# Where the first sums of the down weights stand in the gate/up tiles of a Winograd feed-forward kernel

## The chip, the cores and the metric

The kernel runs as one program on one core of a Trainium2 chip. The metric is the device time of one execution in microseconds (us); the time quoted for a kernel is the median of its runs. TensorE (PE in the profile) does the matrix products, VectorE (DVE) and GpSimd (POOL) do elementwise work, ScalarE (ACT) does copies and activation functions, and SyncE (SP) issues nearly all of the loads and stores. Each engine has one queue and works through it in order; an instruction whose data is not there holds up all that stand behind it on its engine.

## The reference

Two layers (DEPTH = 2) of a hybrid encoder, on 1040 tokens (16 meta tokens and 1024), width 1024, in float32. Each layer is a mixer (gated DeltaNet heads and short convolutions) and then a SwiGLU feed-forward block. Only the second is touched here:

```python
def swiglu(h, w_gate_up, w_down):
    gate, up = jnp.split(h @ w_gate_up.astype(h.dtype), 2, axis=-1)
    return (jax.nn.silu(gate) * up) @ w_down.astype(h.dtype)

for l in range(DEPTH):
    h = h + hybrid_mixer(rmsnorm(h, norm1_w[l]), ...)
    h = h + swiglu(rmsnorm(h, norm2_w[l]), w_gate_up[l], w_down[l])
h = rmsnorm(h, final_norm_w)
return h[:, N_META:]
```

The inner width D_FF is 2816, or 22 tiles of 128 (FT = 22).

## The kernel before

**Number format and products.** Every float32 operand is split into a high part `hi` (rounded to fp32r, by ACT) and a low part `lo` (the rest, by DVE or POOL), and a product is three matmuls per 128 x 128 block: hi x hi, hi x lo, lo x hi. Both feed-forward products are done with one level of Winograd's form of Strassen's method: seven products of half size in place of eight, with sums and differences of weight blocks on one side and of activation blocks on the other.

**Gate/up stage.** The loop `for f in range(FT)` (from L1279) makes one of 22 rows of the inner activation per turn; such a turn is called a tile here. A tile loads four weight blocks of 128 x 512: A11 and A12 into `raw` buffers (2 in all), A21 and A22 into `rw` buffers (tag `ck2`, 5 buffers in all), L1281 to L1284. DVE makes s1t = A21 + A22 (L1289), s2t = s1t - A11 (L1290), then s2t = A12 - s2t (L1293) and A21 = A11 - A21 (L1294); s1t and s2t take `ck2` buffers as well. `w_op` splits each of the seven operands (ACT at L1047, POOL at L1048) into a ring of seven slots. PE does the seven products (p1 to p7, L1065 to L1067); DVE takes the results out of the banks at L1313 (p5), L1324 (p3), L1327 (p6), L1331 (p7) and L1340 (p4). The row is then finished: POOL multiplies the gate by the norm factor (L1354), DVE multiplies up by it (L1355), ACT does the silu (L1356), DVE does the last product (L1357), SP stores the row (L1358), and for rows 4 to 12 DVE makes a difference that SP stores too (L1360, L1361). In layer 0 a product is done in two halves of 260 columns, in layer 1 (the last) in one piece of 512. Tiles 0 to 3 have had two of their products done ahead and do the other five.

**First sums of the down weights.** The down product, which comes next, needs for twelve blocks n = 0 to 11 (128 x 384) the Winograd sum S1 = A21 + A22 of the down weights, then S2 and S3 made from it in place. The S1 sums are done while gate/up runs. `s_under(f)` stands in tile f after the `w_op` calls: tiles 8 to 17 have one sum each (n = f - 8), tile 21 has n = 10 and 11. It calls `s_sum("S1", ...)`, which issues two loads of 192 KB (`a_load`, L1130) into a room and the DVE addition into the sum's home (L1156).

- For n < 8 the room is the two halves of one row, `dw["S", 4]`; all eight sums use it, one after another.
- For n of 8 and above the first load goes to the sum's own home and the second (called o below) to a `ck2` buffer.
- The homes: n = 0 to 5 are in the rows of tag `Y[1]` which held the gate rows of tiles 0 to 2; n = 6, 7 are in a `c` buffer which held a row of tile 3; n = 8, 9 are in `dw["S", 4]` itself; n = 10, 11 are in the row that holds the gate of tile 20.

**What sets the order.** Nothing is placed in the queues by hand. The framework lists the program, and a scheduler that plays a timeline of its own fills each engine's queue: among the instructions whose inputs and buffers are free in that timeline it takes the one that stands first in the program. So an instruction can be put far ahead of its place in the program when nothing it needs holds it back. `after(a, b)` adds a dependency of a on b, and with it a bound on how early a can be taken. The dependencies are kept on the chip by semaphores; the order within each queue is fixed.

Of the kernel before, what the change touches and what calls it, by code (L numbers as in the profile page):

```python
# [11 lines left out]
ALU = mybir.AluOpType  # L12
# [8 lines left out]
FT = 22  # L21
# [21 lines left out]
def trunk(ctx: ExitStack, tc: tile.TileContext, xT, w_in, w_ba, w_out, w_gu, w_dn,  # L43
# [8 lines left out]
    def nm(p):  # L52
        cnt[0] += 1
        return f"{p}_{cnt[0]}"
# [4 lines left out]
    def row(tag, dt=F32, bufs=1):  # L59
        return sb.tile([128, L], dt, tag=tag, bufs=bufs, name=nm(tag))  # L60

    def t2k(tag):
        return sb.tile([128, 4, 128], F32, tag="ck2", bufs=5, name=nm(tag))
# [25 lines left out]
    def after(ins, prev):  # L89

        if prev is not None:
            tc.add_manual_dep(ins.ins, prev.ins.name, dep, reason="order")
        return ins
# [6 lines left out]
    tt = nc.vector.tensor_tensor  # L100
# [116 lines left out]
    S = [(("a0", "a1", "a2"), "a3"), (("b0", "b1", "b2"), "b3")]  # L217
# [62 lines left out]
    for l in range(DEPTH):  # L280
# [788 lines left out]
        def raw4(tag):  # L1069
            if tag == "raw":  # L1070
                return wp.tile([128, WK, 128], F32, tag="raw", bufs=2, name=nm("raw"))
            return t2k("rw")
# [43 lines left out]
        dw, held = {}, {}  # L1116
        at, read_out = [0], {}

        def behind(ins):

            return after(ins, read_out.get(at[0] - 2))
# [6 lines left out]
        def a_load(to, dh, fh, n):  # L1128
            f0 = NF + NP * fh + 3 * (n // 4)
            dma(to.rearrange("p (k e) -> p k e", k=3), w_dn[l, 4 * dh + n % 4, :, f0:f0 + 3, :])  # L1130
            return to
# [11 lines left out]
        def s_room():  # L1143

            nr[2] += 1
            r = nr[2] // 2 % 4
            if ("X", r) not in dw:
                dw["X", r] = row(X[1], F32, 3) if r < 3 else row(Y[1] + "f")
            return dw["X", r][:, 384 * (nr[2] % 2):384 * (nr[2] % 2) + 384]

        def s_sum(which, n, room=None):

            S = s_raw(n)
            if which == "S1":
                r, o = room or (s_room(), s_room())
                tt(out=S, in0=a_load(r, 1, 0, n), in1=a_load(o, 1, 1, n), op=ALU.add)  # L1156
            elif which == "S2":
                behind(tt(out=S, in0=S, in1=a_load(s_room(), 0, 0, n), op=ALU.subtract))
            else:
                behind(tt(out=S, in0=a_raw(1, 1, n), in1=S, op=ALU.subtract))  # L1160

        def s_under(f):

            if f == FT - 1:
                ns = (10, 11)
            else:
                ns = (f - 8,) if 0 <= f - 8 < 10 else ()
            for n in ns:
                S = s_raw(n)
                if n == 0:  # L1170
                    s_raw(6)
                    s_raw(8)
                if n < 8:
                    s_sum("S1", n, (dw["S", 4][:, 0:384], dw["S", 4][:, 384:768]))
                else:
                    s_sum("S1", n, (S, raw4("ck2").rearrange("p a b -> p (a b)")[:, 0:384]))

        def w_unit(u):

# [71 lines left out]
        for n in range(12):  # L1251
            under[n + 3].append(lambda n=n: s_sum("S2", n))
            under[n + 49].append(lambda n=n: s_sum("S3", n))
# [25 lines left out]
        for f in range(FT):  # L1279
# [16 lines left out]
            for n, a in ([("S3", A21), ("A22", A22), ("S4", s2t), ("A12", A12)] if end else  # L1296
                         [("S4", s2t), ("S3", A21), ("A12", A12), ("A22", A22)]):
                if f >= NE or n != "A12":
                    W[n] = w_op(a)
            s_under(f)  # L1300
            g, u = early[f] if f < NE else (row((X[1], Y[1])[f % 2] + "f"), row(X[1], F32, 3))
            ps = {}

# [49 lines left out]
            gv, uv, rv = g[:, o0:L], u[:, o0:L], ss[:, o0:L]  # L1353
            ptt(out=gv, in0=gv, in1=rv, op=ALU.mult)  # L1354
            tt(out=uv, in0=uv, in1=rv, op=ALU.mult)  # L1355
            act(out=gv, in_=gv, func=AF.Silu)  # L1356
            tt(out=uv, in0=uv, in1=gv, op=ALU.mult)  # L1357
            dma(ad[f][:, o0:L], uv)  # L1358
            if NF <= f < NF + NP:
                tt(out=gv[:, 0:NB].rearrange("p (g e) -> p g e", g=2), in0=half(uv, 1), in1=half(uv, 0), op=ALU.subtract)  # L1360
# [46 lines left out]
        for u, (p, b, m) in enumerate(UNITS):  # L1407
# [16 lines left out]
            for j in range(NJ):  # L1424
# [9 lines left out]
                if b == NBK - 1:  # L1434
                    dh, z, op = TO[p]
# [138 lines left out]
```

## Time and profile before

| what | us |
|---|---|
| median of 3 runs | 2581.15 |
| lowest, highest of these | 2574.96, 2581.61 |
| the profiled execution, its time | 2581.81 |
| the profiled execution, its span | 2580.0 |
| mean granted TensorE clock | 0.992 |
| layer 0: first and last store of a finished row (L1358) | 676.0, 1098.8 |
| layer 1: first and last store of a finished row (L1358) | 1956.1, 2356.1 |
| layer 0: S1 sums n = 0 to 7 on DVE (L1156) | 676.3 to 728.3 |
| layer 1: the same | 1957.7 to 2013.2 |
| layer 0: S1 sums n = 8, n = 9 start | 949.4, 970.2 |
| layer 1: S1 sums n = 8, n = 9 start | 2212.2, 2231.9 |

The table gives times from the span's start except in its first five rows. In the rows of a view, the first number is the start in us, the second the time taken, then the engine, the line, the operation, output and inputs with their shapes; in square brackets stands how long the engine had been idle before it and what it had waited for. SPq, PEq and so on are the engines' queues (loads, stores, semaphores). Names are those of the buffers: `a` and `b` are the large buffers of the two halves of the memory plan, which change their part from layer to layer; `rw` is a `ck2` buffer.

### The profile page before, as it was taken

The numbers are of one execution on the slowest core, as the hardware profiler recorded it, in microseconds if no ns is written. First come the engines' busy times: TensorE is split into PE (matmuls) and PEld (weight loads), VectorE is DVE, ScalarE is ACT, GpSimd is POOL, SyncE is SP. The second block draws the span as 40 slices with busy tenths as digits, with TensorE's granted clock in tenths as the row PEclk, the third lists the DMA queues.
The fourth block names the chain that finished last, engine by engine and source line by source line (L and its number), as shares of the span: only waits on it lengthen the run. The fifth ranks groups of instructions, "written<-read, shape, count | busy, mean of one in ns | idle before, by whom it ended". The sixth has DMA issues, their size and how long they took to land. (4 is left out here: it accounts for less than half of the span.)

```text
span 2580.0 us, 45319 instructions
## 1 busy us (share of the span) xinstructions
PE 2501.8 (97%) x17508; PEld 2284.7 (89%) x17508; DVE 1660.6 (64%) x2461; ACT 1045.1 (41%) x1945; POOL 1138.4 (44%) x869
## 2 busy tenths in 40 slices
PE   8999999999999999999999998999998999999998
PEld 6989899998899999999998987999977778887787
DVE  4678423648766666678656884235597776768664
ACT  5664232435233333444445742224452333334444
POOL 2141212325666666655420312212466676675663
PEclk9999999999999999999999999999999999999999
DMA  3445665524432222574323556556343322228631
GB/s 127 137 154 171 210 190 165 195 75 130 136 109 87 88 82 81 193 233 140 96 92 122 173 169 209 171 166 204 106 135 115 117 90 94 87 88 268 188 119 70
DMA packets 213764, 360.04 MB, mean 140 GB/s; under 512 B 25460, under 2 KB 87868, under 8 KB 213548
## 3 DMA queue, kind: packets, MB, share of 16 engines
q1 hardware_dynamic: 180300, 310.17, 36.6%
q10 hardware_dynamic: 31072, 42.61, 5.3%
q0 software_dynamic: 2176, 4.36, 0.5%
q8 instruction: 137, 2.24, 0.4%
q14 instruction: 79, 0.65, 0.1%
HBM read 266.60 MB, written 90.46 MB: 138 GB/s over the span
## 5 line engine op out<-in xcount | busy, mean ns | idle before, releaser
L131 POOL TENSOR_TENSOR wlo<-raw,whi 128x512 fp32r<-128x512 f32 x132 | 176.8, 1341 | 760.1 <-ACT whi L130 666.3
L157 PE MATMUL pacc<-a,whi 128*128 128x346 f32 (+1 forms) x808 | 263.9, 330 | 8.8 <-ACT whi L130 6.5
L159 PE MATMUL pacc<-a,wlo 128*128 128x346 f32 (+1 forms) x808 | 264.8, 329 | 0.5 <-DVE wlo L131 0.3
L157 PE MATMUL pacc<-b,whi 128*128 128x346 f32 (+2 forms) x672 | 235.4, 351 | 0.1
L159 PE MATMUL pacc<-b,wlo 128*128 128x346 f32 (+2 forms) x672 | 233.2, 348 | 0.2 <-POOL wlo L131 0.2
L158 PE MATMUL pacc<-a,whi 128*128 128x346 f32 (+1 forms) x688 | 227.1, 330 | 0.6 <-DVE a L178 0.3
L130 ACT ACTIVATE whi<-raw 128x512 fp32r<-128x512 f32 x168 | 105.2, 628 | 277.3 <-PE pacc L158 158.6
L158 PE MATMUL pacc<-b,whi 128*128 128x346 f32 (+2 forms) x580 | 200.9, 347 | 0.3 <-DVE b L906 0.3
L1048 POOL TENSOR_TENSOR wlo<-rw,whi 128x512 fp32r<-128x512 f32 x92 | 134.7, 1466 | 71.8 <-ACT whi L1047 70.4
L157 PEld LDWEIGHTS pacc<-a,whi 128*128 128x128 f32 x808 | 153.4, 191 | 13.2 <-ACT whi L130 8.2
L159 PEld LDWEIGHTS pacc<-a,wlo 128*128 128x128 f32 x808 | 154.2, 191 | 2.1 <-POOL wlo L131 0.5
L157 PEld LDWEIGHTS pacc<-b,whi 128*128 128x128 f32 x672 | 127.1, 189 | 12.0 <-issue 3.1
L158 PEld LDWEIGHTS pacc<-a,whi 128*128 128x128 f32 x688 | 131.4, 191 | 5.2 <-issue 3.3
L1048 POOL TENSOR_TENSOR a<-rw,a 128x512 fp32r<-128x512 f32 x64 | 105.5, 1651 | 68.3 <-ACT a L1047 68.2
L159 PEld LDWEIGHTS pacc<-b,wlo 128*128 128x128 f32 x672 | 127.3, 190 | 9.4 <-issue 0.8
L1048 POOL TENSOR_TENSOR b<-rw,b 128x512 fp32r<-128x512 f32 x64 | 92.4, 1446 | 84.2 <-ACT b L1047 50.1
L158 PEld LDWEIGHTS pacc<-b,whi 128*128 128x128 f32 x580 | 109.8, 189 | 7.5 <-DVE b L906 0.6
L1047 ACT ACTIVATE whi<-rw 128x512 fp32r<-128x512 f32 x92 | 57.8, 630 | 144.4 <-DVE rw L1293 82.5
L1294 DVE TENSOR_TENSOR rw<-raw,rw 128x512 f32<-128x512 f32 x44 | 98.9, 2247 | 1.2
L1289 DVE TENSOR_TENSOR rw<-rw,rw 128x512 f32<-128x512 f32 x44 | 68.2, 1550 | 48.2 <-POOL wlo L1048 30.9
L1048 POOL TENSOR_TENSOR wlo<-raw,whi 128x512 fp32r<-128x512 f32 x50 | 79.0, 1583 | 32.5 <-ACT whi L1047 32.2
L1047 ACT ACTIVATE b<-rw 128x512 fp32r<-128x512 f32 x64 | 40.3, 630 | 122.3 <-PE pacc L1066 35.2
(970 smaller groups left out, 8439.3 us busy)
## 6 DMA issues: line engine op xcount, KB each, us to landing
raw<-in_w_in SPq DMA_DIRECT2D x112, 256.0 KB
raw<-in_w_gu SPq DMA_DIRECT2D x104, 256.0 KB
rw<-in_w_gu SPq DMA_DIRECT2D x88, 256.0 KB
rw<-in_w_dn SPq DMA_DIRECT2D x94, 192.0 KB
rec<-aqd SPq DMA_DIRECT2D x62, 256.0 KB
rec<-vkd SPq DMA_DIRECT2D x61, 256.0 KB
raw<-in_w_out SPq DMA_DIRECT2D x48, 256.0 KB
b<-ad SPq DMA_DIRECT2D x45, 260.0 KB
```

The costliest lines, as they stand in the source:

```text
L130: whi_done[0] = act(out=hi, in_=raw[:, 0:kk, :], func=AF.Copy)
L131: (tt if lov[0] else ptt)(out=lo, in0=raw[:, 0:kk, :], in1=hi.bitcast(F32), op=ALU.subtract)
L157: mm(ps[:, :n], wh, xh[:, n0:n1], start=(k == 0), stop=False)
L158: mm(ps[:, :n], wh, xl[:, n0:n1], start=False, stop=False)
L159: mm(ps[:, :n], wl, xh[:, n0:n1], start=False, stop=(k == K - 1))
L1047: act(out=hi, in_=src, func=AF.Copy)
L1048: ptt(out=lo, in0=src, in1=hi.bitcast(F32), op=ALU.subtract)
L1289: tt(out=s1t, in0=A21, in1=A22, op=ALU.add)
L1294: tt(out=A21, in0=A11, in1=A21, op=ALU.subtract)
```

## The change

The S1 addition is taken out of `s_sum` and put behind the row. `s_under(f)` keeps the place of the two loads in the program (after the tile's `w_op` calls, ahead of its products) and hands back a list of the additions. These are traced after the row's last product (L1357 of before), with a dependency on it (`row_done`); in tile 21 the dependency is on the last product of row 20 (`row_before`). The rooms, the homes, the number of loads and the number of additions are the same.

```diff
--- before.py
+++ after.py
@@ -1148,13 +1148,10 @@
                 dw["X", r] = row(X[1], F32, 3) if r < 3 else row(Y[1] + "f")
             return dw["X", r][:, 384 * (nr[2] % 2):384 * (nr[2] % 2) + 384]
 
-        def s_sum(which, n, room=None):
+        def s_sum(which, n):
 
             S = s_raw(n)
-            if which == "S1":
-                r, o = room or (s_room(), s_room())
-                tt(out=S, in0=a_load(r, 1, 0, n), in1=a_load(o, 1, 1, n), op=ALU.add)
-            elif which == "S2":
+            if which == "S2":
                 behind(tt(out=S, in0=S, in1=a_load(s_room(), 0, 0, n), op=ALU.subtract))
             else:
                 behind(tt(out=S, in0=a_raw(1, 1, n), in1=S, op=ALU.subtract))
@@ -1165,15 +1162,20 @@
                 ns = (10, 11)
             else:
                 ns = (f - 8,) if 0 <= f - 8 < 10 else ()
+            adds = []
             for n in ns:
                 S = s_raw(n)
                 if n == 0:
                     s_raw(6)
                     s_raw(8)
                 if n < 8:
-                    s_sum("S1", n, (dw["S", 4][:, 0:384], dw["S", 4][:, 384:768]))
+                    r, o = dw["S", 4][:, 0:384], dw["S", 4][:, 384:768]
                 else:
-                    s_sum("S1", n, (S, raw4("ck2").rearrange("p a b -> p (a b)")[:, 0:384]))
+                    r, o = S, raw4("ck2").rearrange("p a b -> p (a b)")[:, 0:384]
+                a_load(r, 1, 0, n)
+                a_load(o, 1, 1, n)
+                adds.append((S, r, o))
+            return adds
 
         def w_unit(u):
 
@@ -1297,7 +1299,7 @@
                          [("S4", s2t), ("S3", A21), ("A12", A12), ("A22", A22)]):
                 if f >= NE or n != "A12":
                     W[n] = w_op(a)
-            s_under(f)
+            adds = s_under(f)
             g, u = early[f] if f < NE else (row((X[1], Y[1])[f % 2] + "f"), row(X[1], F32, 3))
             ps = {}
 
@@ -1354,7 +1356,10 @@
             ptt(out=gv, in0=gv, in1=rv, op=ALU.mult)
             tt(out=uv, in0=uv, in1=rv, op=ALU.mult)
             act(out=gv, in_=gv, func=AF.Silu)
-            tt(out=uv, in0=uv, in1=gv, op=ALU.mult)
+            row_done = tt(out=uv, in0=uv, in1=gv, op=ALU.mult)
+            for to, r, o in adds:
+                after(tt(out=to, in0=r, in1=o, op=ALU.add), row_done if f < FT - 1 else row_before)
+            row_before = row_done
             dma(ad[f][:, o0:L], uv)
             if NF <= f < NF + NP:
                 tt(out=gv[:, 0:NB].rearrange("p (g e) -> p g e", g=2), in0=half(uv, 1), in1=half(uv, 0), op=ALU.subtract)
```

## The prediction

> **What bounds the kernel now.** I read the first part of the page, then the busy time by windows, then in the two gate/up stages the timelines of PE, DVE and SP side by side.
>
> ```profile
> PE 2501.8 (97%) x17508; PEld 2284.7 (89%) x17508; DVE 1660.6 (64%) x2461; ACT 1045.1 (41%) x1945; POOL 1138.4 (44%) x869
> ...
> 650.00:740.00 90.00, 82.50 (x673) 81.05 (x673) 68.26 (x93) 26.16 (x42) 56.51 (x34) 1.00 0.39 128
> 740.00:1050.00 310.00, 304.38 (x2509) 301.42 (x2508) 198.56 (x251) 102.12 (x180) 198.25 (x121) 1.00 0.26 87
> ...
> 1940.00:2020.00 80.00, 76.20 (x319) 60.62 (x319) 60.24 (x57) 23.18 (x36) 56.16 (x32) 0.98 0.38 122
> 2020.00:2320.00 300.00, 298.65 (x1289) 241.54 (x1288) 213.04 (x180) 98.62 (x159) 206.27 (x124) 1.00 0.27 93
> ```
>
> In a row of windows the columns after the length are the busy time of PE, weight loads, DVE, ACT and POOL. PE is the bound, so only a time in which PE stands still can be won or lost. It stands still for 90.00 - 82.50 = 7.50 us at the start of gate/up in layer 0, for 80.00 - 76.20 = 3.80 us at that of layer 1, and in the long rest of the stages for 5.62 of 310 and 1.35 of 300. The eight sums n = 0 to 7 of each layer lie in just these starts, though they belong to tiles 8 to 15: the scheduler has pulled them ahead. Part of the idle time is theirs:
>
> ```profile
> L1156 DVE TENSOR_TENSOR b<-S x6: 546/918/1634, 676.3 to 712.1; 128x384 f32<-128x384 f32 x6
>   DMA S<-in_w_dn: 15.0, 7
> ...
> 676.00:732.00 56.00, 7.79 (x8) 1.00 0.47 152
> 1957.00:2014.00 57.00, 7.61 (x8) 1.00 0.43 140
> ```
>
> The last two rows are windows of line 1156 alone: 16 sums took 15.40 us, 0.96 each. Besides, DVE waited 15.0 us in seven places for a sum's load, in front of all that stood behind the sum.
>
> **What is removed, wait by wait.** First PE's idle times while sums run, then the DVE rows that end them:
>
> ```profile
> 683.34 0.39 PE L1065 MATMUL pa<-P,a 128*128 128x260 f32 x1 [0.85 <-DVE b L1327]
> 697.74 0.39 PE L1065 MATMUL pacc<-a,whi 128*128 128x260 f32 x1 [1.54 <-DVE a L1331]
> 699.73 0.36 PE L1065 MATMUL pacc<-b,a 128*128 128x260 f32 x1 [0.28 <-DVE c L1313]
> 713.01 0.39 PE L1065 MATMUL pf<-a,a 128*128 128x260 f32 x1 [1.33 <-DVE c L1331]
> 735.97 0.39 PE L1065 MATMUL pb<-a,a 128*128 128x260 f32 x1 [1.39 <-DVE a L1331]
> ...
> 1973.73 0.50 PE L1065 MATMUL pa<-a,b 128*128 128x512 f32 x1 [1.24 <-DVE c L1313]
> 1979.20 0.51 PE L1065 MATMUL pf<-b,whi 128*128 128x512 f32 x1 [1.98 <-DVE b L1331]
> ```
>
> ```profile
> 681.55 0.86 DVE L1156 TENSOR_TENSOR b<-S 128x384 f32<-128x384 f32 x1 [2.25 <-DMA S<-in_w_dn]
> ...
> 697.61 1.63 DVE L1156 TENSOR_TENSOR b<-S 128x384 f32<-128x384 f32 x1
> ...
> 712.07 0.55 DVE L1156 TENSOR_TENSOR b<-S 128x384 f32<-128x384 f32 x1
> ...
> 1962.96 0.56 DVE L1156 TENSOR_TENSOR a<-S 128x384 f32<-128x384 f32 x1 [3.01 <-DMA S<-in_w_dn]
> ...
> 1975.33 1.54 DVE L1156 TENSOR_TENSOR a<-S 128x384 f32<-128x384 f32 x1
> ```
>
> Layer 0. The sum at 681.55 held DVE for 2.25 + 0.86 us; behind it stood the L1327 that PE waited for at 683.34: 0.85 is the sum's. The sum at 697.61 stood right before the L1313 of 699.73: 0.28. The sum at 712.07 stood right before the L1331 of 713.01: of 1.33 its own 0.55. The waits of 1.54 and 1.39 had no sum close before them; I give them nothing. Layer 1. After the sum that waited 3.01 us, DVE had no idle time until both PE waits had ended, so 1.24 and 1.98 are its backlog and the next sum's 1.54. A last wait of 3.80 - 1.24 - 1.98 = 0.58 us stands behind a sum of 0.55: 0.55. Sum of the gain: 0.85 + 0.28 + 0.55 + 1.24 + 1.98 + 0.55 = 5.45 us. Bounds: nothing, if another late instruction (a weight load, a POOL split) ends the same waits; and all idle time from the first sum on, 0.85 + 1.54 + 0.28 + 1.33 + 1.39 + 3.80 = 9.19 us, if the loads also stop delaying the weight loads behind them on SP.
>
> **What is added: one sum behind each of rows 8 to 17.** Its loads have by then been there for most of a tile, so DVE doesn't wait for them; it pays the 0.96 us. In layer 0 the tiles repeat exactly, in layer 1 roughly:
>
> ```profile
> 844.18 0.68 DVE L1360 TENSOR_TENSOR b3f<-a 128x520 f32<-128x520 f32 x1
> 846.18 0.43 DVE L1313 TENSOR_TENSOR a<-pf,a 128x260 f32<-128x260 f32 x1 [1.32 <-PE pf L1067]
> ...
> 2106.26 0.68 DVE L1313 TENSOR_TENSOR b<-pacc,b 128x512 f32<-128x512 f32 x1
> 2108.70 0.69 DVE L1331 TENSOR_TENSOR b<-pacc,b 128x512 f32<-128x512 f32 x1 [1.76 <-PE pacc L1067]
> ...
> 2119.35 2.21 DVE L1357 TENSOR_TENSOR b<-b,a3f 128x1024 f32<-128x1024 f32 x1
> ...
> 2127.70 0.68 DVE L1331 TENSOR_TENSOR b<-pf,b 128x512 f32<-128x512 f32 x1
> ...
> 2128.52 0.47 PE L1065 MATMUL pf<-b,b 128*128 128x512 f32 x1 [0.67 <-DVE b L1331]
> ```
>
> In layer 0 DVE has 1.32 us to spare right behind a row (846.18), more than 0.96: nothing lost. In layer 1 most rows have 1.76 us before the L1331 that matters. One (row 9, 2119.35) has none: DVE runs without a break into an L1331 that PE already waits 0.67 us for, so its sum costs 0.96. Bounds for all twenty sums: nothing, and 20 x 0.96 = 19.2 us if each lies on PE's path. I take 0.96.
>
> **Moved: the loads, past SP's queue, and the rooms.** For n < 8 the room is shared, so the loads of tile f + 1 now can't go before row f's sum. They stand behind the row's store on SP, which waits for the same row, so weight loads behind them wait about one sum more: nothing, as those have half a tile. For n = 8, 9 the buffer o counts:
>
> ```profile
> 946.95 0.33 SPq L1130 DMA_DIRECT2D rw<-in_w_dn  x1
> 948.05 0.33 SPq L1358 DMA_DIRECT2D ad<-a  x1
> 951.12 0.33 SPq L1282 DMA_DIRECT2D rw<-in_w_gu  x1
> ...
> 968.85 0.33 SPq L1358 DMA_DIRECT2D ad<-a  x1
> ...
> 949.43 1.66 DVE L1156 TENSOR_TENSOR S<-S,rw 128x384 f32<-128x384 f32 x1 [1.07 <-DMA rw<-in_w_dn]
> ```
>
> The stores at 948.05 and 968.85 are those of rows 14 and 15, 20.8 us apart; the load of o for tile 16 goes then, two rows ahead, and the weight load that would have had the buffer follows the sum's end (949.43 + 1.66 = 951.09). After the change o is kept until row 16 is done: two tiles long one of five `ck2` buffers is missing, and for about one tile two are, when tile 17's o has come in. I followed the buffers by the order in which they are freed. Layer 0: each sum or load comes one release later, and all seven splits still find their operand in time. Layer 1 is tighter; tile 18's s1t then has to wait for the buffer freed at 2253.89 instead of being ready at 2239.47:
>
> ```profile
> 2253.89 0.33 SPq L1283 DMA_DIRECT2D rw<-in_w_gu  x1
> ...
> 2252.76 2.18 DVE L1355 TENSOR_TENSOR b<-b,rstd 128x1024 f32<-128x1024 f32 x1
> 2254.97 1.23 DVE L1357 TENSOR_TENSOR b<-b,b3f 128x1024 f32<-128x1024 f32 x1
> 2257.44 1.72 DVE L1289 TENSOR_TENSOR rw<-rw,rw 128x512 f32<-128x512 f32 x1
> ...
> 2265.06 0.69 DVE L1313 TENSOR_TENSOR b<-pacc,b 128x512 f32<-128x512 f32 x1
> ...
> 2264.77 0.63 ACT L1047 ACTIVATE whi<-rw 128x512 fp32r<-128x512 f32 x1
> ...
> 2266.08 1.29 POOL L1048 TENSOR_TENSOR wlo<-rw,whi 128x512 fp32r<-128x512 f32 x1
> ```
>
> The s1t would run behind L1355, from 2254.94 for 1.72 us. From the start of ACT's split to the end of POOL's the rows have 2264.77 to 2267.37, so 2.60 us later, at 2259.3, S1 is split. PE's p5 of that tile ends by 2265.06 and takes 12 matmuls of 300/1289 = 0.23 us, so it starts by 2262.3: 3.0 us are left. I cost the held buffers at nothing; that cover of 3.0 us is what hides them, and the rival below prices its loss. Tile 21's two sums keep their bound (row 20), and their 0.54 us each stay in a stretch where PE does not wait: nothing.
>
> **The sum.** -5.45 + 0.96 = -4.5 us. The profiled execution took 2581.81 (its span of 2580.0 and 1.8 around it), so 2577.3 for it; it lies 0.7 above the median of 2581.15, which becomes 2576.7. I say 2577.
>
> **The rivals.**
>
> *All the start's idle time goes.* The loads take SP time and memory bandwidth among the weight loads: DMA is at 0.39 there against 0.26 later. Then -9.2, or with the whole idle time of both windows 7.50 + 3.80 = 11.3: 2572 and 2570. Against it: 1.54 and 1.39 follow weight sums, not loads of the down weights.
>
> *Nothing is won.* The PE waits end on other late work, or the first eight sums were filler and the scheduler fills the gap with other early work; as much is paid behind the rows: 2581 to 2583. For it: DVE still waits for weight loads and for POOL in the same stretch, and two PE waits there have no sum near them.
>
> *The held buffers stop the weights* (slower). Place: tiles 18 and 19 of each layer, s1t and s2t waiting for o. It decides where S1 of tile 18 is split later than 2262.3 in layer 1, that is if its buffer comes one release later than worked out; the next one in the trace is the end of tile 18's S4 or of row 16's sum, up to 10 us on. With the 3.0 us used up, 10 - 3.0 = 7.0 us for one tile; for two tiles in two layers 28, less 4.5: 2605; for one tile in each layer 14 - 4.5 = 9.5: 2591. For it: the freed buffers are taken at once (L1282 0.03 us after the sum at 951.12). Against it: the release order as worked out keeps 3.0 us.
>
> *The sums cost their time in every tile of layer 1.* Where DVE and POOL run together the shape that takes 546 ns takes up to 1634 (the sum at 949.43, 1.66 us), and a sum between a row and the next weight sums would push the splits as well: 10 x 0.96 = 9.6 - 5.45 = 4.2: 2585. Against it: the 1.76 us of most rows. [...]
>
> **How the numbers follow.** The three runs of before lie 6.6 us apart, so below 0.3% (7.7 us) a difference is not told from none. Chances: the forecast 0.52 (own range 2573 to 2581), all idle time gone 0.15, nothing won 0.11, held buffers 0.15, sums exposed in layer 1 0.07. Faster by over 0.3% means under 2573.4: most of the second case and the lower edge of the first, 0.17. Slower by over 0.3% means over 2588.9: most of the held buffers, 0.14. Same: 0.69. The range goes from 2570 (11.3 us won) to 2591 (buffers late for one tile in each layer); all twenty sums exposed, with the gain, would be 2581.15 + 19.2 - 5.45 = 2594.9 and is left out.
>
> **What would show it.** Right: the sums n = 0 to 7 stand at rows 8 to 15, each behind its L1357, without a wait for their loads; PE's idle time falls to about 5 us in the first window and about nothing in the second; layer 0's rows keep their distance of 20.8 us. The rivals show as a first window with idle time under 3 us; as an unchanged idle time with other releasers; and as L1289 of tile 18 and 19 waiting for a buffer, with PE waiting for ACT or POOL (L1047, L1048) near the store of row 17. I am wrong if the weights' order in the queues has changed so that the regular tiles cost more or less than 20.8 us each.

## The result, and the profile after

| | before | changed |
|---|---|---|
| median, 22 runs each, us | 2576.77 | 2566.76 |
| lowest, highest | 2568.55, 2583.59 | 2565.20, 2573.96 |
| profiled execution, its time (span) | 2581.81 (2580.0) | 2567.49 (2565.7) |

The ratio of the times is 0.9964, with an interval of 0.9956 to 0.9972: about 10 us less, or 0.36%. The three runs that were known ahead had a median of 2581.15, 4.4 us above that of the 22 runs taken now.

The changed kernel's time by windows, with the columns as before (busy time of PE, weight loads, DVE, ACT, POOL; clock; share and GB/s of DMA). The windows keep the times of before. The changed trace is some 5 us ahead at the first of them and some 14 at the last, so a row of one and a row of the other cover almost the same work.

```profile
650.00:740.00 90.00, 86.47 (x717) 85.88 (x716) 62.05 (x85) 27.75 (x45) 59.93 (x36) 1.00 0.30 103
740.00:1050.00 310.00, 305.83 (x2527) 303.51 (x2526) 190.79 (x259) 102.13 (x180) 195.80 (x121) 1.00 0.29 95
1050.00:1100.00 50.00, 48.10 (x397) 47.48 (x396) 41.32 (x56) 20.52 (x39) 28.90 (x20) 1.00 0.86 287
1940.00:2020.00 80.00, 79.75 (x345) 64.36 (x344) 57.01 (x54) 26.05 (x40) 57.03 (x34) 1.00 0.29 99
2020.00:2320.00 300.00, 295.72 (x1274) 238.51 (x1273) 200.89 (x188) 98.79 (x159) 197.26 (x125) 1.00 0.32 106
```

PE's idle time fell from 7.50 to 3.53 us at the start of gate/up in layer 0 and from 3.80 to 0.25 at that of layer 1. In the long rest it fell a little in layer 0 (5.62 to 4.17) and rose in layer 1 from 1.35 to 4.28. The end of layer 0's gate/up (third row) has 1.90 us of idle time in this trace, and none in that of before. So something was won in three of the five windows and given back in two.

The additions by their line, L1361 now, in the changed kernel (ns of the shortest, median and longest, then the first and last start in us):

```profile
L1361 DVE TENSOR_TENSOR b<-S x6: 541/541/542, 814.6 to 918.7; 128x384 f32<-128x384 f32 x6
L1361 DVE TENSOR_TENSOR a<-S x6: 558/1053/2746, 2084.7 to 2189.4; 128x384 f32<-128x384 f32 x6
...
  DMA a3f<-in_w_dn: 1.6, 1
```

They stand one to a tile, in rows 8 to 15 for n = 0 to 7, and only once did DVE wait for one of their loads. In layer 0 these six take 541 or 542 ns each; in layer 1 the same shape takes from 558 to 2746 ns.

And PE's waits that matter, from its timeline (L1315 is L1313 of before, L1333 is L1331, L1342 is L1340):

```profile
691.80 0.39 PE L1065 MATMUL pacc<-a,whi 128*128 128x260 f32 x1 [1.44 <-DVE a L1333]
703.69 0.39 PE L1065 MATMUL pacc<-b,whi 128*128 128x260 f32 x1 [0.81 <-DVE a L1315]
...
1079.52 0.39 PE L1436 MATMUL pf<-P,b 128*128 128x260 f32 x1 [1.03 <-DVE a L1342]
...
2114.17 0.47 PE L1065 MATMUL pf<-b,b 128*128 128x512 f32 x1 [1.76 <-DVE b L1333]
2193.51 0.47 PE L1065 MATMUL pf<-b,b 128*128 128x512 f32 x1 [1.56 <-DVE b L1333]
```

The wait of 1.54 at 697.74 is still there as 1.44. Those of 0.85, 0.28, 1.33 and 1.39 are gone and one of 0.81 is new. In layer 1's start the 1.24 is gone, the 1.98 has become 0.25, and a third, of 0.59 at 1993.76, is gone too; row 9's wait has grown from 0.67 to 1.76 and row 13 has a new one of 1.56.

**Where the time went, at equal matmul numbers.** Both kernels issue 17,508 matmuls, so I took the start of the k-th matmul in each trace, counted from the first, and looked at how the difference to the trace of before changes from one k to the next. That tells what a stretch of work won or lost, whatever happened ahead of it. A minus is time won, in us. The changed kernel was profiled a second time (run after_again, below), which is the second column.

| stretch | matmuls | changed | changed, again |
|---|---|---|---|
| ahead of gate/up of layer 0 | 0 to 4900 | -4.23 | -5.27 |
| layer 0, start | 4900 to 5600 | -4.27 | -4.29 |
| layer 0, rows 5 to 13 | 5600 to 7300 | 0.00 | +0.02 |
| layer 0, rows 14 to 19 | 7300 to 8200 | -2.18 | -2.18 |
| layer 0, tile 21 and start of down | 8200 to 9000 | +1.23 | -1.33 |
| down of layer 0, mixer of layer 1, first matmuls of gate/up | 9000 to 14720 | -1.95 | -0.79 |
| layer 1, start | 14720 to 15100 | -4.20 | -4.21 |
| layer 1, row 9 | 15300 to 15500 | +1.08 | +1.07 |
| layer 1, rows 12 to 15 | 15700 to 16000 | +1.75 | +1.77 |
| layer 1, rows 16 to 19 | 16000 to 16300 | +0.67 | +0.67 |
| layer 1, rest with its down stage | 16300 to 17507 | -1.92 | -2.29 |

The first row can't come from the change: PE, DVE, ACT and POOL carry out the same instructions in the same order there, and all eleven traces taken beside that of before are 2.5 to 5.9 us ahead of it at matmul 4900. The last row has a gain in ten of the eleven, also where the additions stand as before. Both are differences between executions. What repeats and belongs to the change is -4.28 and -2.18 in layer 0 and, in layer 1, -4.21 with +1.07, +1.77 and +0.67: -7.2 in all. The rest up to the 10 us of the medians isn't located.

A wait that went won more here than the figure in its brackets. At equal matmul numbers the 0.85 and the 1.39 of layer 0's start are worth 1.11 and 1.68 us, and a regular 0.40 there is worth 0.68: about 0.3 us more each. A part of it can be seen in the kernel before: the first matmul behind these waits takes 0.39 us, the next ones 0.28.

### The profile page after: what moved, and what is told of

Same layout as the page of the kernel before. It is cut to its first block, busy times and chain, and to the rows that moved or that the text cites. A ratio compares the mean times of both kernels' runs of the same rounds, so it can differ in the third digit from the quotient of the medians.

```text
span 2565.7 us, 45312 instructions
## 1 busy us (share of the span) xinstructions
PE 2495.7 (97%) x17508; PEld 2282.1 (89%) x17508; DVE 1625.2 (63%) x2461; ACT 1045.3 (41%) x1945; POOL 1126.7 (44%) x869
## 5 line engine op out<-in xcount | busy, mean ns | idle before, releaser
L1291 DVE TENSOR_TENSOR rw<-rw,rw 128x512 f32<-128x512 f32 x44 | 59.4, 1349 | 51.8 <-POOL wlo L1048 29.7
L1296 DVE TENSOR_TENSOR rw<-raw,rw 128x512 f32<-128x512 f32 x44 | 84.3, 1916 | 1.0
```

Source lines behind the costliest of these rows:

```text
L1291: tt(out=s1t, in0=A21, in1=A22, op=ALU.add)
L1296: tt(out=A21, in0=A11, in1=A21, op=ALU.subtract)
```

## The experiments

Each was profiled, and is compared with the trace of before at equal matmul numbers. The table has the stretches that matter, in us; the sections below read them. (The 4.9 us that some expectations give for layer 1's start count from matmul 14600 in the first profile; the second has 4.2 from there too.)

| run | layer 0 start | rows 14 to 19 | tile 21 | layer 1 start | row 9 | rows 12 to 15 | rows 16 to 19 |
|---|---|---|---|---|---|---|---|
| e1_first8 | -4.23 | -0.96 | -0.91 | -4.21 | +1.11 | +1.77 | +0.02 |
| e2_89 | -0.10 | -2.29 | -1.18 | +0.95 | 0.00 | -0.03 | +0.67 |
| e3_ones | +3.46 | 0.00 | -0.38 | +3.49 | +0.01 | 0.00 | 0.00 |
| e4_twice | -4.24 | -2.29 | +2.14 | -4.21 | +3.75 | +4.28 | +2.05 |
| e6_adds_early | -2.32 | +0.05 | +0.06 | +1.64 | +0.79 | -0.03 | +0.04 |
| e8_loads_early | -4.34 | -2.18 | -1.09 | -1.73 | +1.11 | +1.77 | +0.67 |
| e9_last_now | -4.16 | -2.19 | -1.35 | -3.53 | +1.11 | +1.77 | +0.66 |
| e5_p7 | -4.51 | -1.87 | -1.11 | -4.21 | 0.00 | -0.03 | +0.03 |
| e5_again | -4.27 | -1.93 | -1.29 | -4.21 | +0.01 | -0.03 | +0.03 |

### The first eight sums alone (e1_first8)

```diff
-                adds.append((S, r, o))
+                if n < 8:
+                    adds.append((S, r, o))
+                else:
+                    tt(out=S, in0=r, in1=o, op=ALU.add)
```

> Only the sums n = 0 to 7 stand behind their rows; n = 8 to 11 as in the kernel before. Theory A (two effects: the starts of gate/up win 4.3 and 4.9 us because the first eight sums leave them; the order around rows 14 to 19 and tile 21 changes through n = 8 to 11): counted at the same matmuls, PE keeps the gain at both starts (4 to 5 us each) and the loss of 1 us at row 9 of layer 1, and loses the 2.2 us gained in rows 15 to 19 of layer 0; in all 6 to 8 us below the kernel before. Rival B (everything comes from the first eight): equal to the changed kernel within 1 us, the 2.2 us included.

Median 2569.44, ratio 0.9965 (0.9948 to 0.9981): the whole effect within the error. The starts of both layers win as in the changed kernel, and rows 9 and 13 of layer 1 lose as there, so both belong to the sums n = 0 to 7. The loss at rows 16 to 19 of layer 1 is gone, and 1.2 of the 2.2 us won at rows 14 to 19 of layer 0: these come from n = 8 and 9. The other 0.96 is won with the first eight alone; the two don't add up, for n = 8 and 9 alone win 2.29 (next run).

### Sums 8 and 9 alone (e2_89)

```diff
-                adds.append((S, r, o))
+                if n in (8, 9):
+                    adds.append((S, r, o))
+                else:
+                    tt(out=S, in0=r, in1=o, op=ALU.add)
```

> Only the sums n = 8 and 9 stand behind their rows; the others as in the kernel before. Theory A: the starts are as before; layer 0 wins about 2 us in rows 14 to 19, because the held buffers move the weight sums away from the L1331 that PE waits 0.40 us for in every tile; layer 1 loses 0 to 2 us there. In all within 0 to 2 us below before. Rival B: no change against before anywhere (within 0.5 us at the same matmuls).

Median 2575.94, ratio 0.9997 (0.9982 to 1.0011): nothing that the times can tell. In the trace there are two small effects of opposite sign, -2.29 in layer 0 and +0.67 in layer 1. By windows, this kernel:

```profile
650.00:740.00 90.00, 83.34 (x682) 82.09 (x681) 67.99 (x91) 26.84 (x43) 56.35 (x34) 1.00 0.40 129
740.00:1050.00 310.00, 305.91 (x2528) 303.60 (x2527) 189.11 (x251) 101.90 (x180) 195.66 (x121) 1.00 0.26 87
```

The start's idle time is nearly that of before (6.66 against 7.50). Layer 1's start shows +0.95. The waits of 1.24 and 1.98 are as before (1.99 now); behind them stands a stretch of lowered clock (1.55 us lost, read in the last section), and PE, late by that, no longer meets the third wait of 0.59, which wins 0.87. The second window has PE busy 305.91, as in the changed kernel (305.83; before 304.38). The `ck2` buffers held by o are what differs here: DVE's weight sums move relative to the evacuations, and the wait for L1331 of 0.40 us that every regular tile of layer 0 had (14 of them before, the last at 1046.39) is absent in rows 14 to 19, but for one of 0.50 in the changed kernel and of 0.40 in this one. That the held buffers cause the shift is read from the traces and not shown; no run held a buffer without moving a sum.

### Additions early without waiting for loads (e3_ones)

```diff
-                tt(out=S, in0=a_load(r, 1, 0, n), in1=a_load(o, 1, 1, n), op=ALU.add)
+                a_load(r, 1, 0, n)
+                a_load(o, 1, 1, n)
+                if n < 8:
+                    k = ones.unsqueeze(1).to_broadcast([128, 3, 128])
+                    tt(out=S.rearrange("p (k e) -> p k e", k=3), in0=k, in1=k, op=ALU.add)
+                else:
+                    tt(out=S, in0=r, in1=o, op=ALU.add)
```

The kernel is that of before, but the additions n < 8 read a constant in place of their loads; the sums are left out of the computation.

> The kernel before, but the additions n = 0 to 7 read a constant tile instead of what they load (the sums are left out of the computation); loads and additions are both still early. Theory A1 (the cost is DVE standing still for the loads, 15 us in seven places): with the waits gone the starts win most of what the change wins, 3 us or more of the 4.3 and of the 4.9 at the same matmuls. Rival A2 (the additions' own 0.96 us each or the loads' traffic and SP time is the cost): the starts win 1 us or less.

One run: 2581.09, beside a median of 2577.73 for before. The starts became 3.46 and 3.49 us slower, not faster. With nothing waiting for the loads, the scheduler issued them in bursts. SP's timeline (x is how many loads in the row), and the PE wait that follows, in this kernel:

```profile
651.32 5.44 SPq L1130 DMA_DIRECT2D S<-in_w_dn  x4
658.44 9.16 SPq L1130 DMA_DIRECT2D S<-in_w_dn  x7
668.13 8.48 SPq L1130 DMA_DIRECT2D S<-in_w_dn  x7
...
671.51 0.58 PE L1065 MATMUL pb<-b,a 128*128 128x260 f32 x1 [3.61 <-DVE a L1346]
```

Eighteen loads held SP for 23 us. Most of it is waiting, by an estimate from the kernel before: there issuing a load into this room took 0.38 us at the median of 36, and 18 x 0.38 = 6.8 us. Weight loads had to stand between and behind them: in this kernel's lines, the weight load L1289 went out only at 667.73 and L1290 at 676.71. Of layer 0's loss 1.5 us is the lowered clock that followed PE's wait of 3.61 us (0.50 over 3.4 us): from the first matmul behind it to the start of the 15th after that it took 3.38 us, and 1.90 behind the wait of 1.39 in the kernel before. In layer 1 PE's waits are 0.56, 1.28 and 2.81 us, together 0.84 more than before; most of the 3.49 is the lowered clock there (0.61, 0.50 and 0.89 in three windows of 3.4 us): behind the wait of 2.81 the same 15 steps took 6.41 us, behind that of 1.98 in the kernel before 3.59, so 2.8 us. So this run did not take the wait away and leave the rest; it made another kernel. What it shows is that the sums had paced their own loads: taking a wait out can let something worse through.

### Each of the first eight sums twice (e4_twice)

```diff
-                after(tt(out=to, in0=r, in1=o, op=ALU.add), row_done if f < FT - 1 else row_before)
+                for _ in range(2 if f < 16 else 1):
+                    after(tt(out=to, in0=r, in1=o, op=ALU.add), row_done if f < FT - 1 else row_before)
```

> The changed kernel with each addition behind rows 8 to 15 done twice (same result). Prices a sum behind a row. Theory: layer 0 has room (1.3 us idle behind a row, 0.55 to 1.1 us needed) and stays within 0.5 us of the changed kernel at the same matmuls from row 8 to row 15; layer 1 pays at rows 9 and 13 alone, about 1 us more each, 2 us. Rival (sums are exposed in every tile of layer 1): 8 x 0.5 to 1 us = 4 to 8 us more in layer 1.

One run: 2579.32, against 2577.73 for before. In layer 0, matmuls 5600 to 7300, the extra sums cost 0.01 us: they lie wholly in DVE's idle time. In layer 1 they cost in two places. PE's waits there in this kernel:

```profile
2117.64 0.47 PE L1065 MATMUL pf<-b,b 128*128 128x512 f32 x1 [2.87 <-DVE b L1333]
2180.80 0.77 PE L1065 MATMUL pb<-b,b 128*128 128x512 f32 x1 [2.79 <-DVE b L1333]
```

The first is row 9, which pays 3.75 - 1.08 = 2.67 us for its second sum; about 1.4 of it lies behind the wait, where seven matmuls in a row start 0.42 or 0.43 us apart, in place of 0.23. The second stands a row earlier than the loss of the changed kernel's row 13: row 12 is exposed now, by 2.79 us and a lowered clock behind it (0.53 over 3.4 us; the first matmul takes 0.77 us in place of 0.47), together 4.3; row 13, with PE that much later, then pays nothing. Rows 8, 10 and 11 pay nothing with two sums each. Two more losses lie where this kernel has single sums or none: +2.05 in rows 16 to 19, 1.4 more than in the changed kernel, and +1.44 behind matmul 16300, where the ten other traces win. What makes these isn't shown. So the rival that the sums are exposed in every tile of layer 1 falls. Whether a tile pays hangs on how late PE is when it comes there.

### Additions early, their loads late (e6_adds_early)

```diff
-                a_load(r, 1, 0, n)
-                a_load(o, 1, 1, n)
-                adds.append((S, r, o))
+                if n < 8:
+                    k = ones.unsqueeze(1).to_broadcast([128, 3, 128])
+                    tt(out=S.rearrange("p (k e) -> p k e", k=3), in0=k, in1=k, op=ALU.add)
+                    adds.append((r, o, n))
+                else:
+                    a_load(r, 1, 0, n)
+                    a_load(o, 1, 1, n)
+                    tt(out=S, in0=r, in1=o, op=ALU.add)
...
-            for to, r, o in adds:
-                after(tt(out=to, in0=r, in1=o, op=ALU.add), row_done if f < FT - 1 else row_before)
+            for r, o, n in adds:
+                for fh, to in enumerate((r, o)):
+                    after(a_load(to, 1, fh, n, True), row_done)
```

> The additions n = 0 to 7 stay early but read a constant (the sums are left out of the computation); their sixteen loads are issued behind rows 8 to 15; n = 8 to 11 as before. Theory L (the loads cost: what stands early on SP and in memory delays the weight loads, and DVE waits for them): the starts win as in the changed kernel, 4 us or more each. Rival D (the additions' own time on DVE costs): they win 1.5 us or less each, the changed kernel's further 2.5 to 3.5 us being the additions' 7.7 us of DVE time.

One run: 2579.55, beside 2579.08 for before. With the additions in the start but no loads and no waits for loads, layer 0 wins 2.32 of the 4.27, and neither of the two theories holds there. So, as far as the scheduler's order is the same, about 1.95 us is the price of the additions' own place on DVE, and about 2.3 goes with the loads and DVE's waiting for them. In layer 1 the start is 1.64 us slower than before. DVE's and PE's timelines of this kernel show how:

```profile
1972.92 3.10 DVE L1177 TENSOR_TENSOR a<-ones 128x384 f32<-128x384 f32 x2
1975.95 1.75 DVE L1300 TENSOR_TENSOR rw<-raw,rw 128x512 f32<-128x512 f32 x1
1977.62 0.68 DVE L1338 TENSOR_TENSOR b<-pf,b 128x512 f32<-128x512 f32 x1
...
1978.35 0.79 PE L1065 MATMUL pf<-b,whi 128*128 128x512 f32 x1 [2.80 <-DVE b L1338]
```

Freed of their loads, the additions come in pairs; 3.10 us of them and 1.75 of a weight sum stand in front of the evacuation that PE waits 2.80 us for. Before had 1.98 there. Behind the wait the clock is lowered (0.51 over 3.4 us): from the first matmul there to the start of the 14th after it 4.79 us went by, and 3.36 behind the wait of 1.98 in before, so 1.4 us is lost, most of the whole loss. Without it, layer 1's start would be about as in before: PE's waits are 1.28 + 2.80 = 4.08 us, against 3.81, though no load is near.

Row 9 of layer 1 loses 0.79 in this kernel with no sum behind it. There too DVE has no break between the row and the evacuation; that stretch took longer here with other instructions, and PE's wait grew from 0.67 to 1.47. So the row's place is exposed to whatever lengthens the stretch, a sum being one case.

### The loads' traffic put back into the start (e8_loads_early)

```diff
...
+            if f < 4:
+                for i in range(4):
+                    to = s_raw(8 + i % 2)
+                    after(a_load(to, 1, i % 2, 2 * f + i // 2, True), row_done)
```

Sixteen loads more in the changed kernel, of the same size, four behind each of rows 0 to 3; nothing reads them.

> The changed kernel with sixteen extra loads of down weights of 192 KB each, four behind each of rows 0 to 3, into the room the sums use later; nothing waits for them but later loads of that room (same result). They put back the traffic and SP's queue of before without the additions. Theory L: the starts lose most of the gain again, 2.5 us or more of 4.3 (layer 0) and of 4.9 (layer 1). Rival D: they lose 1 us or less each.

One run: 2570.98, beside 2579.08 for before. This kernel by windows:

```profile
650.00:740.00 90.00, 86.47 (x716) 85.87 (x715) 62.17 (x87) 28.12 (x44) 59.38 (x36) 1.00 0.44 138
1940.00:2020.00 80.00, 77.92 (x334) 62.12 (x333) 55.98 (x56) 25.65 (x39) 60.60 (x34) 1.00 0.42 137
```

DMA's share is 0.44 in layer 0's start, more than before had (0.39), and PE is as busy as in the changed kernel: 86.47. The loads as traffic, and their time on SP, cost nothing there; the 2.3 us that went with them in e6_adds_early are then, by elimination, DVE's waits for them. In layer 1 they cost more than half of what had been won, 4.21 - 1.73 = 2.5 us: PE waits 0.63, 0.67 and 0.77 us for evacuations there, where the changed kernel has one wait of 0.25, and the granted clock stays at 1.00.

### The last two sums put back (e9_last_now)

```diff
-                adds.append((S, r, o))
+                if n < 10:
+                    adds.append((S, r, o))
+                else:
+                    tt(out=S, in0=r, in1=o, op=ALU.add)
```

> The changed kernel with n = 10, 11 added where they were before, at once after their loads. Theory (putting these two behind tile 21's row costs about 2 us in layer 0, where the page of the changed kernel has PE waits of 0.46, 1.03 and 0.41 us that before has not): those waits go, 1.5 to 2.5 us below the changed kernel, counted at the same matmuls from 8300 to 9000. Rival (they come from the other sums' new order): no difference.

Median 2571.38, ratio 0.9975 (0.9964 to 0.9986): not faster than the changed kernel. The trace does have -1.35 in tile 21, where the first trace of the changed kernel had +1.23. That seemed to settle that moving n = 10 and 11 costs 2.5 us, until the second profile of the changed kernel was read (next but one).

### Behind p7 of the same tile (e5_p7)

The losses of row 9 and row 13 come from the place right behind the row, in a stretch where DVE works without a break. p7's evacuation stands later, and between it and the end of the row DVE has time: in each of tiles 8 to 17 of layer 1 it stands idle there for 1.50 us or more in the changed kernel. In this version the additions n < 10 are ordered behind that, and n = 10, 11 are added at once, as in e9_last_now.

```diff
...
-                tt(out=part(u, 1, j), in0=pin(ps["b", j]), in1=part(u, 1, j), op=ALU.add)
+                ps["p7"] = tt(out=part(u, 1, j), in0=pin(ps["b", j]), in1=part(u, 1, j), op=ALU.add)
...
-                after(tt(out=to, in0=r, in1=o, op=ALU.add), row_done if f < FT - 1 else row_before)
+                after(tt(out=to, in0=r, in1=o, op=ALU.add), ps["p7"])
```

> The changed kernel with the additions n = 0 to 9 ordered behind their own tile's p7 (taken out of its bank) instead of behind the row's last product, and n = 10, 11 where they were before. Theory: behind p7 DVE has 1 to 2.6 us idle in every tile of layer 1, so the losses at rows 9 and 13 of layer 1 (1.08 and 1.75 us at the same matmuls) go to under 0.3 each, the gains at the starts stay (4.2 and 4.9), and tile 21 of layer 0 wins 1 to 2 us against the changed kernel: 3 to 5 us below the changed kernel, 13 to 15 below before. Rival (the losses belong to the weights' pace, not to the place of the sum): as the changed kernel within 1 us.

Median 2566.22 against 2579.08 for before, ratio 0.9952 (0.9939 to 0.9966). The run beside which only the place of the sums differs is e9_last_now, on the same chip: 2571.38, 0.9975 (0.9964 to 0.9986). Behind p7 is 5.2 us lower by the medians, and 3.5 lower in the three stretches of layer 1.

### Both versions again, on one chip (after_again, e5_again)

> The changed kernel once more, beside the next one on one chip. Expected from its 22 runs: 0.9964 of before, 10 us; in the profile at the same matmuls as in its first one: starts 4.3 and 4.9 us won, 2.2 in rows 14 to 19 of layer 0, 1.1, 1.7 and -0.7 lost in layer 1.

> Sums n = 0 to 9 behind p7, n = 10, 11 at once, again. By the matmuls of its first profile it wins 7.5 us in gate/up of layer 0 and 4.0 in that of layer 1, against 5.2 and 1.4 of the changed kernel: 4 to 5 us below the changed kernel. Rival: the two are the same in time (within 1.5 us), as their first medians of 2566.2 and 2566.8 have it.

The changed kernel: 2568.66 in 11 runs, ratio 0.9971 (0.9960 to 0.9981). The version behind p7: 2564.28 in 5 runs, ratio 0.9952 (0.9940 to 0.9965). Before had 2577.29. Behind p7 is thus 4.4 us below the change and 13.0 below before by the medians. The two intervals overlap by a little, so by times alone the first of these is likely, not certain. The traces name the place. The window of layer 1 and DVE's rows in row 9 of the version behind p7 (L1336 is p7's evacuation, L1364 the sum):

```profile
2020.00:2320.00 300.00, 298.65 (x1289) 241.75 (x1288) 210.22 (x190) 99.00 (x160) 202.20 (x125) 1.00 0.33 108
...
2111.96 1.68 DVE L1299 TENSOR_TENSOR rw<-raw,rw 128x512 f32<-128x512 f32 x1
2113.56 0.68 DVE L1336 TENSOR_TENSOR b<-pf,b 128x512 f32<-128x512 f32 x1
2114.27 0.92 DVE L1364 TENSOR_TENSOR a<-S 128x384 f32<-128x384 f32 x1
```

PE is busy 298.65 there, exactly as before; the changed kernel has 295.72. The sum now stands behind the evacuation that PE waits for. The 1.07 + 1.77 + 0.67 = 3.5 us are saved.

The second profile of the changed kernel has no idle time at all in the window from 1050 to 1100. DVE's timeline in tile 21 in the first profile, and then the window and the same instruction in the second:

```profile
1069.48 0.56 DVE L1361 TENSOR_TENSOR a3f<-a3f,rw 128x384 f32<-128x384 f32 x1 [1.60 <-DMA a3f<-in_w_dn]
```

```profile
1050.00:1100.00 50.00, 50.00 (x419) 50.00 (x419) 43.68 (x61) 22.44 (x43) 29.29 (x21) 1.00 0.88 300
...
1067.12 0.54 DVE L1361 TENSOR_TENSOR a3f<-a3f,rw 128x384 f32<-128x384 f32 x1
```

In the one DVE waited 1.60 us for the load of n = 11, in the other the load was there. So the order is the same and the cost is 0 or about 2.6 us, by when a load lands. Of the four traces with n = 10, 11 behind the row, the two others are e8_loads_early, which lost nothing there, and e4_twice, which lost 2.14 without such a wait. In e4_twice DVE waited 1.12 and 0.24 us for ACT (L1245) a little later instead, and behind that an instruction of L1155 took 2.83 us; it took 2.79 behind the load's wait above, and 0.55 in the two traces without a loss. So a late DVE is common to both losses; how often it comes stays open.

## Where the prediction was right, and where it failed

**The order.** Right: the sums stand behind rows 8 to 17 and wait for no load (the one wait is in tile 21), and the starts of both layers win. The direction was right; the size was about half: -4.5 forecast, -10 measured by the medians (2581.15 to 2576.7 forecast, 2576.77 to 2566.76 measured). So 0.36% stands just beyond the 0.3% that was called no difference, and 2566.8 below the range's 2570. About 4.4 us of the miss in the absolute time is that three runs stood for before.

**Layer 0's start, 1.68 us: the term that failed most.** It measured 4.3. Its parts at equal matmul numbers, which are the same within 0.01 in both profiles of the changed kernel:

| wait of before | forecast, us won | measured, us won |
|---|---|---|
| 0.85 at 683.34 | 0.85 | 1.11 |
| 1.54 at 697.74 and 0.28 at 699.73 | 0.28 | 0.61 |
| 1.33 at 713.01 | 0.55 | 0.70 |
| 1.39 at 735.97 | nothing | 1.68 |

The other 0.2 lies ahead of the first sum. The step that failed is the wait of 1.39 us: I gave it nothing because no sum stood close before it. It is the sums' by a way round through ACT and POOL. The kernel before, DVE and POOL, and then the same place in the changed kernel (L1295, L1291 and L1333 are L1293, L1289 and L1331 of before):

```profile
724.31 1.43 POOL L1048 TENSOR_TENSOR a<-rw,a 128x512 fp32r<-128x512 f32 x1
727.69 0.56 DVE L1156 TENSOR_TENSOR S<-S 128x384 f32<-128x384 f32 x1 [1.98 <-DMA S<-in_w_dn]
728.17 0.68 DVE L1293 TENSOR_TENSOR rw<-raw,rw 128x512 f32<-128x512 f32 x1
729.66 1.29 POOL L1048 TENSOR_TENSOR wlo<-rw,whi 128x512 fp32r<-128x512 f32 x1 [3.91 <-ACT whi L1047]
730.98 1.77 DVE L1289 TENSOR_TENSOR rw<-rw,rw 128x512 f32<-128x512 f32 x1 [1.33 <-POOL wlo L1048]
735.50 0.42 DVE L1331 TENSOR_TENSOR a<-pb,a 128x260 f32<-128x260 f32 x1
```

```profile
717.19 1.29 POOL L1048 TENSOR_TENSOR a<-rw,a 128x512 fp32r<-128x512 f32 x1
718.52 0.69 DVE L1295 TENSOR_TENSOR rw<-raw,rw 128x512 f32<-128x512 f32 x1 [2.85 <-POOL a L1048]
720.79 1.28 POOL L1048 TENSOR_TENSOR wlo<-rw,whi 128x512 fp32r<-128x512 f32 x1 [2.30 <-PE pacc L1066]
722.11 1.76 DVE L1291 TENSOR_TENSOR rw<-rw,rw 128x512 f32<-128x512 f32 x1 [1.02 <-POOL wlo L1048]
726.65 0.41 DVE L1333 TENSOR_TENSOR a<-pb,a 128x260 f32<-128x260 f32 x1
```

In the changed kernel the weight sum L1295 starts 0.04 us after POOL's split ends (717.19 + 1.29 = 718.48). Before, that split ended at 724.31 + 1.43 = 725.74, but the sum n = 7 stood in DVE's queue, waiting 1.98 us for its load, and L1293 started at 728.17, 2.4 us later. POOL's next split waited for what ACT made of it, L1289 waited for that split, and the L1331 that PE waits for came behind L1289 and L1294. In the changed kernel POOL's split waits for PE in its turn. So DVE's break of 1.33 us in front of L1289 does not part the sum from the late evacuation; it is the sum's delay, come back through two engines. This chain is read from the traces. How the 1.68 divides between the load's wait and the addition isn't shown; e6_adds_early, with additions in the start but no loads, wins 0.88 of it.

The rest of the miss in this term is smaller. I counted the waits by their brackets, and each that went was worth about 0.3 us more. In front of the 1.33 DVE had no break since 702.24, and a load's wait of 1.39 and sums of 0.56, 0.97 and 0.55 us left that stretch, 3.5 us together. Still only 0.70 was won: all of the 1.33 went, but the new wait of 0.81 came 18 matmuls ahead of it. Right was that the 1.54 has another cause: it is still 1.44.

**Layer 1's start, 3.77 us.** It measured 4.21. Right, mechanism and size: PE's three waits fell from 3.81 us together to 0.25 (the 1.98 left that rest), and the other 0.65 would be what the waits were worth beyond their brackets, by an estimate from the 0.3 us each in layer 0.

**Row 9, 0.96 us lost.** It measured 1.07. The place and the size were right, though not by a sum of 0.96: the sum there takes 2.75 us, while the weight sum next to it takes 1.78 where L1289 took 2.88 before.

**Row 13, given nothing.** It measured 1.77 (rows 12 to 15). I looked for rows where PE already waited, and only row 9 had that. The test should have been whether DVE has a break between the row and the L1331 that matters. It has none in row 13 of the kernel before:

```profile
2198.07 2.21 DVE L1357 TENSOR_TENSOR b<-b,a3f 128x1024 f32<-128x1024 f32 x1
2200.20 1.78 DVE L1289 TENSOR_TENSOR rw<-rw,rw 128x512 f32<-128x512 f32 x1
2202.02 2.77 DVE L1294 TENSOR_TENSOR rw<-raw,rw 128x512 f32<-128x512 f32 x1
2204.71 0.68 DVE L1331 TENSOR_TENSOR b<-pf,b 128x512 f32<-128x512 f32 x1
```

The changed kernel's row 13 has a sum of 1.65 us in that chain, at 2189.42, and PE waits 1.56 there.

**The held buffers, nothing.** The feared stall did not come: in rows 14 to 19 of both traces of the changed kernel no wait of PE ends on ACT or POOL. But moving n = 8 and 9 moved the weight sums, which was worth -2.3 us in layer 0 and +0.67 in layer 1 (e2_89, where they alone are moved); that the buffers they hold do it is read from the traces. I had followed when each buffer comes free, and asked only whether a split would be late, not what else on DVE changes its turn.

**Tile 21's sums, nothing.** It was nothing in one trace and about 2.6 in another: I took their loads to be there.

**The rivals.** "All the start's idle time goes" had the nearer size, with the wrong mechanism for layer 0: the loads as traffic cost nothing there (e8_loads_early), and about 2.5 us in layer 1. "Nothing is won" and the held buffers as a brake fell with the trace. The sums in layer 1 do stretch, to 2746 ns, and are exposed in two rows, not in all. The traces show what they ran beside: of the 20 sums n = 0 to 9 of both layers, those that began while POOL was idle took 0.55 or 0.56 us before (11 sums) and 0.54 to 0.56 after the change (13); those that began during an instruction of POOL took 0.86 to 1.66 us (9) and 1.04 to 2.75 (7). The one of 2.75, in row 9, began at 2107.29, 0.51 us after POOL's L1356, which took 2.84 us. What makes them longer, and what POOL loses, wasn't shown.

**What stays open.** How layer 1's gain divides into additions, waits and loads: taking the loads out kept its waits (e6_adds_early), putting loads back took 2.5 us (e8_loads_early), and e6_adds_early and e3_ones changed the scheduler's order as well, so neither took one part away cleanly. And of the 10 us between the medians the traces place 7.2. The lowered clock may be part of the rest (last section): the mean granted clock is 0.9931 over the 46 runs of before that were taken beside the experiments and 0.9941 over the 33 of the changed kernel, and by an estimate 0.001 of 2577 is 2.6 us; on the one chip where both were run it is 0.9935 and 0.9942, or 1.8 us. Whether the change lowers this share, or the chips and executions do, no run shows.

## What to carry to other kernels

A short instruction that a scheduler pulls into a busy stretch as filler cost more here than the wait right behind it: it delayed what followed in its queue, by its load's wait too (the sum n = 7 of layer 0 took 0.56 us behind a wait of 1.98, and the weight sum behind it started 2.4 us after the split of POOL's that it follows at once in the changed kernel). To price its removal, go back from the late instruction to the engine's last break and add up all of it that leaves; that bounds what can be won there. Where that break ended on another engine's work, as DVE's did here on POOL's split, go on back through that engine: the break may itself be the delay. To place it, look for an event of the same tile with a proven break behind it (here p7's evacuation), not for the end of a chain that runs on into the next tile's work. Where two executions of one kernel differ by more than the effect, compare traces at equal instruction numbers and stretch by stretch; and read a second execution before a loss is put down to an order.

## What the runs showed of the hardware

Executions of the kernel before spread over 15 us (2568.55 to 2583.59). Time and mean granted clock go together: of the 46 runs of before that were taken beside the experiments, the four at 0.995 took a mean of 2572.6 us, the 39 at 0.992 to 0.994 one of 2577.8 and the three below 2583.5; of the changed kernel's 22 runs the two at 0.992 took 2570.88 and 2573.96 us, the 15 at 0.994 a mean of 2566.9. Two windows of 3.4 us of the kernel before, then the same two of the changed kernel, whose work is the same there:

```profile
136.00:139.40 3.40, 1.89 (x14) 1.29 (x18) 3.40 (x6) 2.54 (x8) 3.40 (x9) 0.76 0.48 182
139.40:142.80 3.40, 3.40 (x30) 2.34 (x23) 2.00 (x5) 3.37 (x8) 3.40 (x12) 0.74 0.80 246
```

```profile
136.00:139.40 3.40, 2.67 (x28) 1.86 (x29) 3.40 (x7) 3.32 (x11) 3.40 (x12) 1.00 0.60 219
139.40:142.80 3.40, 2.57 (x20) 2.33 (x18) 1.88 (x3) 3.37 (x6) 3.40 (x11) 1.00 0.81 255
```

The granted clock is 0.76 and 0.74 in the one and 1.00 in the other. In windows of 0.1 us, in the kernel before, it is 0.80 from 137.7 to 137.8, 0.50 in each from there to 141.1, 0.64 in the next and 1.00 behind it, so 3.4 us were at 0.50. The same 30 matmuls took 4.38 us there (137.51 to 141.89), behind a PE wait of 2.31 us, and 2.83 in the changed kernel (136.73 to 139.56), behind one of 1.47: 1.55 us were lost in one of the two executions. In gate/up, too, a lowered clock stands behind PE waits in these traces. In e6_adds_early, behind the wait of 2.80 us, and in the kernel before at the same place, behind 1.98 us:

```profile
1974.60:1978.00 3.40, 0.94 (x5) 0.42 (x3) 3.40 (x3) 0.51 (x1) 2.54 (x2) 1.00 0.67 202
1978.00:1981.40 3.40, 3.05 (x7) 2.47 (x8) 3.33 (x5) 0.00 (x0) 1.71 (x1) 0.51 0.00 1
```

```profile
1974.60:1978.00 3.40, 2.62 (x12) 1.82 (x10) 3.37 (x3) 0.63 (x1) 3.40 (x3) 1.00 0.41 158
1978.00:1981.40 3.40, 2.20 (x9) 1.80 (x10) 2.67 (x5) 0.00 (x0) 1.67 (x1) 1.00 0.62 191
```

Where PE worked for 0.94 us of the first window, the clock is 0.51 in the second; where it worked for 2.62, it stays at 1.00. But it isn't the wait's length alone. In e2_89 PE waits the same there, 1.99 us, and this follows:

```profile
1977.72 0.50 PE L1065 MATMUL pf<-b,whi 128*128 128x512 f32 x1 [1.99 <-DVE b L1336]
...
1978.00:1981.40 3.40, 3.40 (x11) 2.71 (x11) 1.85 (x3) 0.00 (x0) 1.25 (x2) 0.65 0.57 198
1981.40:1984.80 3.40, 3.40 (x14) 2.69 (x14) 2.61 (x2) 2.00 (x3) 3.03 (x2) 0.84 0.21 67
```

So behind one and the same PE wait of 2 us the clock was lowered in one execution and not in another. From the first matmul behind the wait to the start of the 14th after it, e2_89 took 4.91 us and the kernel before 3.36, so 1.55 us were lost; in the lowered stretch the matmuls start 0.43 us apart, elsewhere 0.23. What sets the clock down behind one wait and not behind another, no run shows. The waits ahead of the lowered clock in these traces of layer 1 were 1.99 us (e2_89), 2.79 (e4_twice), 2.80 (e6_adds_early) and 2.81 (e3_ones); behind that of 1.98 in the kernel before it was 1.00.
